# Side work of a two-layer kernel told out at other points of its feed-forward stage: from the gate/up blocks into the first down-projection

## The chip, the cores and the metric

The kernel runs on one core of one Trainium2 chip. The metric is the device time of one execution in microseconds (us), lower is better. Five engines are named as in the profile: PE (TensorE matmul; PEld its weight loads), DVE (VectorE), ACT (ScalarE), POOL (GpSimd) and SP (SyncE, which here issues the DMA transfers).

## The reference, cut to what matters

Two transformer layers run one after the other on 512 tokens of width 1024. The change lies in the feed-forward part of the first layer and in two pieces of the second layer that depend on no activation:

```
# first layer, feed-forward part, width 2816
h = rms_norm(x, ffn_norm)
x = x + (silu(h @ w_ffn_gate) * (h @ w_ffn_up)) @ w_ffn_down
...
# second layer: modulation, three rows of 1024 from the conditioning vector c
mod = silu(c) @ w_ada + b_ada
shift, scale, gate = split(mod, 3)
# second layer: matrices of the state-space mixer, from its parameters alone
lam_bar = exp(lam * dt); b_bar = ((lam_bar - 1) / lam) * b; ...
```

The kernel calls the first piece `modulation()` and the second `s5_params()`. Both are needed only after the feed-forward part: scale and shift in its last normalization, the gate and the matrices later.

## The kernel before, in words

All large products use a three-matmul split: an f32 operand becomes a rounded part (hi) and a remainder (lo), and hi·hi, hi·lo and lo·hi are summed in PSUM (`mm3`, lines 177 to 179). A weight tile is fetched by SP (line 198), cast by ACT to its hi part (line 206) and reduced by POOL to its lo part (line 207). There are three raw buffers and three pairs of hi and lo buffers.

The feed-forward part is cut in two halves of 11 column blocks, 22 blocks m in all (lines 1400 to 1414). One block multiplies the normalized activations hT by 128 columns of the gate weight and by 128 of the up weight, 24 matmuls each, into two of the four PSUM banks tagged `mm`. ACT takes the tanh of the gate bank (line 1405), DVE forms the silu from it (line 1406, the last read of the gate bank), DVE multiplies by the up bank (line 1408, the last read of that bank), and a split writes gT (hi by ACT at line 187, lo by DVE at line 188). After each half a down-projection adds gT times 11 x 128 rows of the down weight to XT: two column blocks of 512 columns, in each of them 11 values of k, for each k the four token tiles t with one bank each, three matmuls per tile. So a column block is 132 matmuls and needs all four `mm` banks at its start. DVE adds the four banks to XT at its end (line 1225). The first half's down-projection is the `add_proj` of line 1414 (through `proj_tok`, line 253), the second's is called later, with a normalization behind it.

Two generators tell out the side work in steps; `some(gen, n)` runs n steps at the point of the program where it is called.

- `modulation()` (line 1270) has 25 steps. For each of three rows n and eight values of k it fetches a 512 KB tile `aw` of w_ada (line 1283, one buffer) and lets DVE multiply and add it into `am` (line 1285 for k = 0, line 1287 for the others, one buffer); call these the products. The step after a row's eighth product first closes that row: `am` is split into two parts in buffers tagged `t4k` (three buffers, lines 184 and 185), PE sums the partitions with four narrow matmuls (line 1295, banks `tp`), DVE adds the bias (line 1296, buffers `t2k`), and SP stores the result to `modd`. Row 0 is closed in step 9, row 1 in step 17, row 2 in step 25.
- `s5_params()` (line 1310) has 11 steps for each of two halves of the groups, 22 in all: Bb, BD and Cm (with four PE transposes of line 1327); two steps of CL; the matmuls of line 1350 with Kp; two steps that copy a table `tk` (t4k buffers) out; two steps of E with one of ET behind each (eight PE transposes of line 1378); and PH, a chain of some forty small DVE products. Nearly all of its DVE work has line 1096 (`cmul`).

Before the change every block m runs one step of `s5_params()` and one step of `modulation()`, two of the latter in blocks 10, 11 and 12 (lines 1411 and 1412). For m < 4 an `issue_after` keeps that work's DVE instructions behind the last one of the normalization ahead of the stage.

The program is written as one sequence. A planner at compile time then puts each instruction in the fixed queue of its engine: an instruction may go ahead of earlier ones as soon as its inputs and its buffer are free by the planner's estimate, and of several that could go, the one written first goes first. Buffers that share a tag (`t2k`, `t4k`, `tp`, `mm`) are handed out by turns. On the chip each engine works through its queue in order and waits by semaphores.

Of the kernel before, what the change touches and what calls it, by code (L numbers as in the profile page):

```python
# [25 lines left out]
NT = 4  # L26
# [62 lines left out]
def row(ap, off, n, parts=128):  # L89
    return bass.AP(tensor=ap.tensor, offset=ap.offset + off, ap=[[0, parts], [1, n]])  # L90
# [60 lines left out]
def tile_hybrid(ctx: ExitStack, tc: tile.TileContext, I, out):  # L151
# [9 lines left out]
    def mm_ps():  # L161
        return ps.tile([128, 512], FT, tag="mm", bufs=4, name="mm")
# [4 lines left out]
    def tp_ps():  # L167
        return ps.tile([128, 512], FT, tag="tp", bufs=2, name="tp")

    def t2k(dt=FT):  # L170
        return at.tile([128, 512], dt, tag="t2k", bufs=4, name="t2k")
# [4 lines left out]
    def mm3(o, a, b, first, last):  # L176
        nc.tensor.matmul(o, a[0], b[0], start=first, stop=False)  # L177
        nc.tensor.matmul(o, a[0], b[1], start=False, stop=False)  # L178
        nc.tensor.matmul(o, a[1], b[0], start=False, stop=last)  # L179

    def split(p, hi, lo, scale=1.0):

        if isinstance(scale, float) and scale == 1.0:
            nc.scalar.copy(hi, p)  # L184
            return nc.vector.tensor_tensor(lo, p, fl(hi), op=OP.subtract)  # L185
        else:
            nc.scalar.activation(hi, p, AF.Copy, scale=scale)  # L187
            return nc.vector.scalar_tensor_tensor(lo, p, scale, fl(hi), op0=OP.mult, op1=OP.subtract)
# [24 lines left out]
    def wl(w, c0, cols, kc=KD, k0=0, dst=None):  # L213
        return wload([(lambda v: v, wcols(w, c0, cols, kc, k0))], kc, cols, dst)

    def proj_t(w, x, kc, m, n0=0, n1=T, bank=mm_ps):

        o = bank()
        for k in range(kc):
            mm3(o[:m, n0:n1], [v[:, k, :m] for v in w], [v[:, k, n0:n1] for v in x], k == 0, k == kc - 1)  # L220
        return o
# [28 lines left out]
            yield  # L250
        return o

    def proj_tok(load, x, kc, kper, cols, tail=0, then=None):


        o = [mm_ps() for _ in range(NT)]
        starts = list(range(0, kc, kper))
        body = len(starts) - tail
        steps = []
        for i, k0 in enumerate(starts):  # L260
            w = load(k0)
            for k in range(k0, min(k0 + kper, kc)):
                steps += [(0 if i < body else 1, k if i < body else t, k, t, w, k - k0) for t in range(NT)]
        for _, _, k, t, w, kw in sorted(steps, key=lambda z: (z[0], z[1])):
            mm3(o[t][:, :cols], [v[:, k, t * 128:(t + 1) * 128] for v in x],
                [v[:, kw, :cols] for v in w], k == 0, k == kc - 1)
            if then and k == kc - 1:
                then(t, o[t])
        return o

    def rsqrt_steps(ss, n, dim, parts=128):
# [35 lines left out]
    def some(gen, n=1 << 30):  # L307
        for _ in range(n):
            if next(gen, gen) is gen:
                return  # L310
# [386 lines left out]
    for j in range(4):  # L697
        w = wl(w_in, C0["iq"] + j * 128, 128)
# [72 lines left out]

    g_q = grow(I["mla_q_norm"], 384)
    o4 = proj_tok(lambda k: wl(w_in, C0["cq"], 384, 2, k), hT, KD, 2, 384)
    todo.add(gates(2))
    for _ in tok_norms(o4, 384, g_q, cqT):
# [6 lines left out]
                 for k in range(3)], 3, 256)  # L782
    qps = [pc.tile([128, T], FR, name=f"qps{h}") for h in range(4)]
    o4 = proj_tok(lambda k: wpe, cqT, 3, 3, 256)
    qpt = []
    qpa = t4k().rearrange("p (t h d) -> p t h d", t=NT, h=4)
# [165 lines left out]
    for h in range(4):  # L952
# [39 lines left out]
        while n <= 256:  # L992
# [23 lines left out]
            if n < 256:  # L1016
                m = 256 // n
# [200 lines left out]
        split(mixed[:, k], *[v[:, k % 4] for v in mx[k // 4]])  # L1218
    mxT = [Rows([m[i] for m in mx], 4) for i in range(2)]

    def add_proj(w, x, kc, tail=0, then=None, last=None):

        for n0 in range(0, D, 512):
            def add(t, o):
                nc.vector.tensor_tensor(XT[:, t, n0:n0 + 512], XT[:, t, n0:n0 + 512], o, op=OP.add)  # L1225
                if then:
                    then(n0 // 512, t)

            proj_tok(lambda k: wl(w, n0, 512, min(2, kc - k), k, last if n0 and k >= kc - 2 else None),
                     x, kc, 2, 512, tail if n0 else 0, add)  # L1230

    hT = hT_tiles()
    g_ffn = grow(I["ffn_norm"], D)
# [23 lines left out]
    w_g, w_u, w_d = I["w_ffn_gate"][0], I["w_ffn_up"][0], I["w_ffn_down"][0]  # L1257
    spare = pmix.tile([128, 2, 2, 1024], FR, tag="mixed", name="spare")
    spare = [[spare[:, i, j] for j in range(2)] for i in range(2)]
    add_proj(I["w_out"][0], mxT, KD, 3, norm_x, spare[1])  # L1260
    first2 = proj_halves([wl(w_g, 0, 128, dst=spare[0]), wl(w_u, 0, 128)], hT)
    stg.close()
# [3 lines left out]
    KH = KF // 2  # L1266
    gT = [pf.tile([128, KH, T], FR, name=f"gT{i}") for i in range(2)]
    modd = dr.tile([24, 128], FT, name="modd")

    def modulation():  # L1270

        cth = pf.tile([128, KD], FT, name="cth")
        nc.scalar.activation(cth, cs, AF.Tanh, scale=0.5)
        nc.vector.scalar_tensor_tensor(cs, cth, 1.0, cs, op0=OP.add, op1=OP.mult)
        nc.vector.tensor_scalar(cs, cs, 0.5, None, op0=OP.mult)
        w_ada = I["w_ada_2"][0].rearrange("(k p) c -> p k c", p=128)
        one = pf.tile([128, 1], FR, name="one")
        nc.vector.tensor_copy(one, ones)
        for n in range(3):
            am = pf.tile([128, D], FT, tag="am", bufs=1, name="am")  # L1280
            for k in range(KD):
                aw = pf.tile([128, 1024], FT, tag="aw", bufs=1, name="aw")
                nc.sync.dma_start(aw, w_ada[:, k, n * D:(n + 1) * D])
                if k == 0:
                    nc.vector.tensor_scalar(am, aw, cs[:, 0:1], None, op0=OP.mult)
                else:
                    nc.vector.scalar_tensor_tensor(am, aw, cs[:, k:k + 1], am, op0=OP.mult, op1=OP.add)  # L1287
                yield
            parts = [at.tile([128, 1024], FR, tag="t4k", bufs=3, name="am") for _ in range(2)]
            split(am, *parts)  # L1290
            for c in (0, 512):
                p, r = tp_ps()[0:1], t2k()[0:1]
                nc.sync.dma_start(r, row(I["b_ada_2"], n * D + c, 512, 1))
                for i, v in enumerate(parts):
                    nc.tensor.matmul(p, one, v[:, c:c + 512], start=i == 0, stop=i == 1)
                nc.vector.tensor_tensor(r, r, p, op=OP.add)
                nc.sync.dma_start(row(modd, n * D + c, 512, 1), r)
# [99 lines left out]
            yield  # L1397

    mod_steps, s5_steps = modulation(), s5_params()
    for half in range(2):  # L1400
        for i in range(KH):
            m = half * KH + i
            pg = proj_t(wl(w_g, m * 128, 128), hT, KD, 128) if m else first2[0]
            th = t2k()
            nc.scalar.activation(th, pg, AF.Tanh, scale=0.5)
            nc.vector.scalar_tensor_tensor(th, th, 1.0, pg, op0=OP.add, op1=OP.mult)  # L1406
            pu = proj_t(wl(w_u, m * 128, 128), hT, KD, 128) if m else first2[1]
            nc.vector.tensor_tensor(th, th, pu, op=OP.mult)  # L1408
            split(th, gT[0][:, i], gT[1][:, i], 0.5)
            with tc.issue_after(at_norm[0].ins) if m < 4 else nullcontext():  # L1410
                some(s5_steps, 1)
                some(mod_steps, 2 if m in (10, 11, 12) else 1)
        if not half:
            add_proj(w_d[:KH * 128], gT, KH)
    some(mod_steps)
    some(s5_steps)
    st5.close()
# [22 lines left out]
    def norm_twice(half, t):  # L1440
# [25 lines left out]
        for k in range(0, KD, 2):  # L1466
# [5 lines left out]
            for kk in range(2):  # L1472
# [3 lines left out]
                at_norm[0] = nc.vector.scalar_tensor_tensor(lo, p[:, kk], sh, fl(hi), op0=OP.add, op1=OP.subtract)  # L1476

    add_proj(w_d[KH * 128:], gT, KH, 3, norm_twice)
    ud = dr.tile([512, T], FT, name="ud")
    us = proj_halves(w_us + [wl(w2, C2["u"] + m * 128, 128) for m in range(2, 3)], h2)  # L1480
# [5 lines left out]
    for t in range(NT):  # L1486
        x = XT[:, t]
# [552 lines left out]
    for n0 in range(0, D, 512):  # L2040
        o4 = proj_tok(lambda k: wl(w_o2, n0, 512, 2, k), mix, 4, 2, 512, n0 // 256)
        for t in range(NT):
# [4 lines left out]
            w = 256 if n0 and t == NT - 1 else 512  # L2047
# [34 lines left out]
```

## Time and profile before

| | us |
|---|---|
| median of 3 runs (lowest to highest) | 1378.11 (1372.89 to 1378.55) |
| profiled execution, its own time | 1378.97 |
| its span, first to last instruction | 1377.2 |
| PE busy | 1279.4 (93%) |
| DVE busy | 858.9 (62%) |
| POOL busy | 640.1 (46%) |
| ACT busy | 551.5 (40%) |

The feed-forward stage with what surrounds it lies at about 600 to 1000 us of the span. The page gives the shares of the engines over the whole span; the views of single stretches (windows, waits by engine, the timeline of one engine) tell which engine waits for which, and where. In a timeline the number in brackets at the end of a row is the idle time of the engine just before, with the instruction that ended it. A busy PE counts matmuls that overlap their neighbours, so the starts of successive matmuls, not their durations, give PE's rate.

### The profile page before, as it was taken

How to read it: one execution, taken by the hardware profiler on the slowest of the kernel's cores; microseconds unless marked ns; L12 is line 12 of the kernel's file. 1: busy time of each engine (PE TensorE's matmuls, PEld its weight loads, DVE VectorE, ACT ScalarE, POOL GpSimd, SP SyncE). 2: the span in 40 equal slices, each digit the busy share in tenths (PEclk: the TensorE clock that was granted, in tenths of full speed). 3: DMA queues.
4: the chain of work that ended last, by engine and by line, in shares of the span. 5: the costliest groups of instructions: out<-in, count | busy, mean ns of one | idle time of the engine just before them, and what ended most of it. 6: DMA issues, size and time to landing. Idle time of an engine off the chain costs nothing. (4 is left out here: it accounts for less than half of the span.)

```text
span 1377.2 us, 18201 instructions
## 1 busy us (share of the span) xinstructions
PE 1279.4 (93%) x6418; PEld 1054.0 (77%) x6418; DVE 858.9 (62%) x1831; ACT 551.5 (40%) x1242; POOL 640.1 (46%) x552
## 2 busy tenths in 40 slices
PE   8989999999989999999998899999989788789998
PEld 6777887777768888878876688887778678677786
DVE  6755897776534346268667516354363758897885
ACT  4554542322234434343423123432343234447772
POOL 3334433333455455554565345554532443547663
PEclk9999999999999999999999899999999898999999
DMA  6252222221423373333765434533325665231233
GB/s 199 71 158 58 63 75 65 62 57 36 116 80 88 86 176 92 123 92 115 224 196 187 143 99 121 169 109 102 113 77 162 185 173 132 69 92 47 77 108 138
DMA packets 201962, 156.16 MB, mean 113 GB/s; under 512 B 27535, under 2 KB 175707, under 8 KB 201869
## 3 DMA queue, kind: packets, MB, share of 16 engines
q1 hardware_dynamic: 201868, 154.98, 38.7%
q8 instruction: 51, 0.84, 0.3%
q14 instruction: 43, 0.34, 0.1%
HBM read 136.58 MB, written 18.37 MB: 113 GB/s over the span
## 5 line engine op out<-in xcount | busy, mean ns | idle before, releaser
L207 POOL TENSOR_TENSOR wlo<-wraw,whi 128x512 fp32r<-128x512 f32 (+4 forms) x388 | 507.1, 1327 | 602.7 <-ACT whi L206 601.4
L206 ACT CAST whi<-wraw 128x512 fp32r<-128x512 f32 (+4 forms) x388 | 212.3, 575 | 366.1 <-issue 217.3
L177 PE MATMUL mm<-hT,whi 128*128 128x512 f32 (+2 forms) x840 | 335.8, 400 | 0.0
L179 PE MATMUL mm<-hT,wlo 128*128 128x512 f32 (+2 forms) x840 | 327.9, 390 | 0.0
L178 PE MATMUL mm<-hT,whi 128*128 128x512 f32 (+2 forms) x840 | 327.7, 390 | 0.0
L179 PEld LDWEIGHTS mm<-hT,wlo 128*128 128x128 f32 x840 | 160.4, 191 | 31.3
L177 PEld LDWEIGHTS mm<-hT,whi 128*128 128x128 f32 x840 | 160.9, 191 | 29.9 <-PE mm L179 0.5
L178 PEld LDWEIGHTS mm<-hT,whi 128*128 128x128 f32 x840 | 161.0, 192 | 28.5 <-issue 0.7
L177 PE MATMUL mm<-whi,gT 128*128 128x512 f32 x176 | 71.7, 408 | 14.5 <-DVE t2k L1406 6.9
L1225 DVE TENSOR_TENSOR XT<-XT,mm 128x512 f32<-128x512 f32 x24 | 16.3, 685 | 99.7 <-PE mm L179 99.6
L178 PE MATMUL mm<-wlo,gT 128*128 128x512 f32 x176 | 71.3, 405 | 0.0
L179 PE MATMUL mm<-whi,gT 128*128 128x512 f32 x176 | 71.2, 405 | 0.0
L177 PE MATMUL mm<-whi,hT 128*128 128x512 f32 (+3 forms) x160 | 60.1, 375 | 0.3 <-ACT hT L184 0.3
L179 PE MATMUL mm<-whi,hT 128*128 128x512 f32 (+3 forms) x160 | 59.3, 371 | 0.9 <-DVE hT L185 0.9
L178 PE MATMUL mm<-wlo,hT 128*128 128x512 f32 (+3 forms) x160 | 59.3, 371 | 0.2 <-POOL wlo L207 0.2
L1287 DVE SCALAR_TENSOR_TENSOR am<-aw,prm,am 128x1024 f32<-128x1024 f32 x21 | 32.4, 1543 | 36.2 <-DMA aw<-in_w_ada_dram 36.2
L185 DVE TENSOR_TENSOR pt4k<-tp,pt4k 128x512 fp32r<-128x512 f32 (+1 forms) x96 | 45.8, 483 | 14.4 <-ACT pt4k L184 13.7
L177 PEld LDWEIGHTS mm<-whi,gT 128*128 128x128 f32 x176 | 34.2, 194 | 24.7 <-DVE t2k L1406 7.3
L184 ACT CAST pt4k<-tp 128x512 fp32r<-128x512 f32 (+1 forms) x96 | 40.1, 421 | 32.0 <-PE tp L387 30.8
L187 ACT ACTIVATE gT<-t2k 128x512 fp32r<-128x512 f32 x22 | 13.9, 631 | 82.3 <-DVE t2k L1408 82.3
L179 PEld LDWEIGHTS mm<-whi,gT 128*128 128x128 f32 x176 | 34.1, 194 | 8.3
L178 PEld LDWEIGHTS mm<-wlo,gT 128*128 128x128 f32 x176 | 34.1, 194 | 7.9
(641 smaller groups left out, 2666.8 us busy)
## 6 DMA issues: line engine op xcount, KB each, us to landing
wraw<-in_w_in_dram SPq DMA_DIRECT2D x70, 512.0 KB
aw<-in_w_ada_dram SPq DMA_DIRECT2D x24, 512.0 KB
wraw<-in_w_ffn_gate_dram SPq DMA_DIRECT2D x22, 512.0 KB
wraw<-in_w_ffn_up_dram SPq DMA_DIRECT2D x22, 512.0 KB
wraw<-in_w_ffn_down_dram SPq DMA_DIRECT2D x20, 512.0 KB
wraw<-in_w_out_dram SPq DMA_DIRECT2D x16, 512.0 KB
PA<-biasd SPq DMA_DIRECT2D x4, 640.0 KB
x<-in_x_dram SPq DMA_DIRECT2D x4, 512.0 KB
```

Of the source, the lines that this page charges most:

```text
L177: nc.tensor.matmul(o, a[0], b[0], start=first, stop=False)
L178: nc.tensor.matmul(o, a[0], b[1], start=False, stop=False)
L179: nc.tensor.matmul(o, a[1], b[0], start=False, stop=last)
L184: nc.scalar.copy(hi, p)
L185: return nc.vector.tensor_tensor(lo, p, fl(hi), op=OP.subtract)
L187: nc.scalar.activation(hi, p, AF.Copy, scale=scale)
L206: nc.scalar.copy(hi[:, d], raw[:, d])
L207: nc.gpsimd.tensor_tensor(lo[:, d], raw[:, d], fl(hi[:, d]), op=OP.subtract)
L1225: nc.vector.tensor_tensor(XT[:, t, n0:n0 + 512], XT[:, t, n0:n0 + 512], o, op=OP.add)
L1287: nc.vector.scalar_tensor_tensor(am, aw, cs[:, k:k + 1], am, op0=OP.mult, op1=OP.add)
```

## The change

In both halves a block runs its steps only if it is not one of the last two of its half (`i < KH - 2`, that is blocks 0 to 8 and 11 to 19). There it runs one step of `s5_params()`, and one of `modulation()` in the second half alone. The first down-projection gets a function that is called after the last token tile of each k: a step of `s5_params()` at k = 1, 5 and 9, and a step of `modulation()` at k = 1 to 10. With two column blocks these are 6 and 20 steps. So the steps of `s5_params()` stand at blocks 0 to 8 (steps 1 to 9), in the down-projection (10 to 15) and at blocks 11 to 17 (16 to 22); those of `modulation()` in the first column block (1 to 10), in the second (11 to 20) and at blocks 11 to 15 (21 to 25). The `issue_after` stays, but it now covers steps of `s5_params()` alone.

```diff
-    def proj_tok(load, x, kc, kper, cols, tail=0, then=None):
+    def proj_tok(load, x, kc, kper, cols, tail=0, then=None, beside=None):
...
             if then and k == kc - 1:
                 then(t, o[t])
+            if beside and t == NT - 1:
+                beside(k)
...
-    def add_proj(w, x, kc, tail=0, then=None, last=None):
+    def add_proj(w, x, kc, tail=0, then=None, last=None, beside=None):
...
-                     x, kc, 2, 512, tail if n0 else 0, add)
+                     x, kc, 2, 512, tail if n0 else 0, add, beside)
...
     mod_steps, s5_steps = modulation(), s5_params()
+
+    def told_down(k):
+        some(s5_steps, 1 if k % 4 == 1 else 0)
+        some(mod_steps, 1 if k else 0)
+
...
             with tc.issue_after(at_norm[0].ins) if m < 4 else nullcontext():
-                some(s5_steps, 1)
-                some(mod_steps, 2 if m in (10, 11, 12) else 1)
+                if i < KH - 2:
+                    some(s5_steps, 1)
+                    some(mod_steps, half)
         if not half:
-            add_proj(w_d[:KH * 128], gT, KH)
+            add_proj(w_d[:KH * 128], gT, KH, beside=told_down)
```

## Rows read from the trace of the kernel before

**Rows 1.** The page, part 1: busy time, share of the span, instructions.

```profile
PE 1279.4 (93%) x6418; PEld 1054.0 (77%) x6418; DVE 858.9 (62%) x1831; ACT 551.5 (40%) x1242; POOL 640.1 (46%) x552
```

**Rows 2.** Waits of PE, 600 to 800 us, then 800 to 980: total, times, longest.

```profile
PE mm L177 <- DVE t2k L1406: 6.9, 1, 6.9
PE mm L177 <- DVE t2k L1408: 3.2, 1, 3.2
...
PE tp L1378 <- DVE E L1096: 2.4, 1, 2.4
PE tp L1378 <- DVE t2k L1296: 1.0, 1, 1.0
...
PE mm L177 <- DVE t2k L1408: 1.5, 1, 1.5
```

**Rows 3.** Windows: stretch, then length; PE, PEld, DVE, ACT, POOL busy; clock, DMA.

```profile
751.67:769.00 17.33, 7.23 (x20) 4.93 (x19) 16.04 (x41) 2.55 (x5) 7.12 (x4) 0.61 0.54 174
...
796.50:824.50 28.00, 28.00 (x121) 22.61 (x120) 0.00 (x0) 5.19 (x10) 11.47 (x9) 1.00 0.34 103
```

**Rows 4.** Timeline of PE at the start of the first down-projection.

```profile
752.84 0.39 PE L179 MATMUL mm<-whi,gT 128*128 128x512 f32 x1
760.10 0.79 PE L177 MATMUL mm<-whi,gT 128*128 128x512 f32 x1 [6.87 <-DVE t2k L1406]
...
764.97 0.79 PE L177 MATMUL mm<-whi,gT 128*128 128x512 f32 x1 [3.23 <-DVE t2k L1408]
...
768.97 0.43 PE L177 MATMUL mm<-whi,gT 128*128 128x512 f32 x1
```

**Rows 5.** Timeline of DVE across the end of the first half.

```profile
747.51 1.28 DVE L1287 SCALAR_TENSOR_TENSOR am<-aw,prm,am 128x1024 f32<-128x1024 f32 x1 [3.25 <-DMA aw<-in_w_ada_dram]
748.72 0.68 DVE L1408 TENSOR_TENSOR t2k<-t2k,mm 128x512 f32<-128x512 f32 x1
...
752.65 1.35 DVE L1287 SCALAR_TENSOR_TENSOR am<-aw,prm,am 128x1024 f32<-128x1024 f32 x1 [2.28 <-DMA aw<-in_w_ada_dram]
...
757.58 1.24 DVE L1096 TENSOR_TENSOR t2k<-PH 128x8 f32<-128x8 f32 x1
...
759.36 0.68 DVE L1406 SCALAR_TENSOR_TENSOR t2k<-t2k,mm 128x512 f32<-128x512 f32 x1
...
764.23 0.68 DVE L1408 TENSOR_TENSOR t2k<-t2k,mm 128x512 f32<-128x512 f32 x1
```

**Rows 6.** Waits of all engines, 625 to 800 us: the products' own row.

```profile
DVE am L1287 <- DMA aw<-in_w_ada_dram: 36.2, 16, 4.9
```

**Rows 7.** Side work against its place in the program: groups by line, and timeline rows.

```profile
L1283 SPq DMA_DIRECT2D aw<-in_w_ada_dram x24: 327/328/413, 630.1 to 781.4; - x24
L1285 DVE TENSOR_SCALAR am<-aw,prm x3: 642/1405/1683, 636.6 to 742.0; 128x1024 f32<-128x1024 f32 x3
L1287 DVE SCALAR_TENSOR_TENSOR am<-aw,prm,am x21: 1273/1286/2310, 647.3 to 786.0; 128x1024 f32<-128x1024 f32 x21
L184 ACT CAST am<-am x3: 1044/1052/1054, 685.3 to 880.1; 128x1024 fp32r<-128x1024 f32 x3
...
630.51 0.43 SPq L1424 DMA_DIRECT2D g_fin<-in_final_norm_dram  x1
...
860.33 1.26 DVE L1296 TENSOR_TENSOR t2k<-t2k,tp 1x512 f32<-1x512 f32 x2
```

**Rows 8.** Timeline of PE around the wait of the transposes in the first half.

```profile
713.34 0.98 PE L1378 MATMUL tp<-ident,E 128*128 128x128 f32 x7 [2.38 <-DVE E L1096]
714.08 0.48 PE L177 MATMUL mm<-hT,whi 128*128 128x512 f32 x1
...
717.76 0.43 PE L177 MATMUL mm<-hT,whi 128*128 128x512 f32 x1
```

**Rows 9.** Timeline of DVE: the additions to XT at both column ends.

```profile
793.71 2.79 DVE L1225 TENSOR_TENSOR XT<-XT,mm 128x512 f32<-128x512 f32 x4 [6.46 <-PE mm L179]
...
824.51 2.79 DVE L1225 TENSOR_TENSOR XT<-XT,mm 128x512 f32<-128x512 f32 x4 [28.01 <-PE mm L179]
```

## The prediction, made before the changed kernel ran

> **What bounds the kernel now.** I read the shares of the engines first: PE is busy for 93% of the span, DVE for 62% [rows 1]. So a change that neither adds nor removes matmuls can only pay where PE waits, and the second view is the list of PE's waits from 600 to 980 us. The reader is to see that those that matter here all name DVE, and that all but one lie in the first half of the feed-forward stage; from 800 to 980 us there is a single one, of 1.5 us [rows 2]. The third view is the table of windows: where the first down-projection starts, PE is busy for 7.23 of 17.33 us at a granted clock of 0.61, a mixture of the two levels 1.2 and 2.4 GHz, while DVE is busy for 16.04 us; in the second column block of the same projection PE is full at clock 1.00 and DVE does nothing for 28 us [rows 3]. Work that crowds DVE at the one place would be free at the other.
>
> The timeline of PE prices the crowding. At full clock matmuls start 0.233 us apart (28.00 us for 120, counting one of the two that straddle an edge [rows 3]). After the matmul at 752.84 the next was due at 753.07; instead twelve matmuls were started from 760.10 on before the one at 768.97, when the rate was back [rows 4]. That is 15.9 us for 12 x 0.233 = 2.8 us of work: **13.1 us lost**, 6.87 + 3.23 = 10.1 in the two waits and 3.0 at the low clock behind them. The two waits are for PSUM banks: the projection's third and fourth bank are the gate and up banks of block 10, free when DVE has read them (lines 1406 and 1408).
>
> The timeline of DVE says why it was late. Ahead of these two reads, at 759.36 and 764.23, its queue holds products that sit waiting for their weights, 3.25 and 2.28 us, and the beginning of PH [rows 5]. Over the stage the products wait 36.2 us in 16 places [rows 6], and whatever stands behind them waits too.
>
> **Does the order follow the program?** Only in part, and the sum hangs on it. The products run far ahead of their place: the last one stands in block 20, after the first down-projection, and ran at 786.0; a transfer written behind the whole stage, g_fin, was issued at 630.51. What takes a buffer shared by turns stays at its place: row 1 was split before row 2's first product at 742.0, but its bias was added at 860.33, by block 13; row 2's products ended at 786.0 + 1.3 = 787.3 and its split came at 880.1 [rows 7]. So moving the calls will not by itself move the products of rows 0 and 1: they will still fill the first half. But row 2's products need `am`, free only when row 1 is split; that needs two of three t4k buffers, two of which row 0 holds until its closing matmuls; and row 0's closing now stands at k = 9 of the first column block, behind block 10 in the turns for t2k and tp. I therefore expect the eight products of row 2 at about 775 to 825, no longer at 742 to 787.
>
> **The change part by part**, against the profiled execution's own 1378.97 us (span 1377.2 us and 1.8 us around it; 0.9 us over the median of 1378.11).
>
> 1. *Row 2's products leave the end of the first half.* From 742.0 to 759.36 DVE loses the product of 742.0 (up to 1.68 us), the waits of 3.25 and 2.28 and the products of 1.28 and 1.35 [rows 5, 7]: 9.8 us. The gate bank of block 10 would be read at 749.5, before PE asks at 753.07: margin 3.5 us, out of which PH, which may still be placed here, needs nothing more than it does now. One more product (1.29) lies between the two reads, so the up bank would be read at 764.23 - 11.1 = 753.1 and be free at 753.8, which is when PE asks for it. Row 0's closing also leaves (two additions, 1.26 us). I take the whole 13.1; the bounds are 0 (another waiting product takes the place) and 13.1.
> 2. *Row 0's closing leaves the first half*: PE's wait of 1.0 us for line 1296 goes [rows 2]. Bounds 0 and 1.0; I take 1.0.
> 3. *PH and row 2's closing leave block 21.* The wait of 1.5 us at the start of the second down-projection goes [rows 2], as both now end by block 17. Bounds 0 and 1.5; I take 1.5.
> 4. *E of step 8.* PE waits 2.38 us for it in mid-half, and then starts nine matmuls in 3.68 us, 1.6 over their 2.1: 4.0 us in all [rows 8]. The step stays at block 7 and the products around it stay too, in a new order. I take 0, with bounds of 4.0 either way.
> 5. *New work beside the down-projection*: steps 10 to 15 and the products. DVE's idle time hides their busy time (all eight products are 10.3 us, against 28 us idle in one column block [rows 3, 7]), but not an ill-placed wait: the four additions to XT at each column end free PE's banks [rows 9], and one of them behind a waiting product holds PE. The mean wait is 36.2 / 16 = 2.3 us, the longest 4.9 [rows 6]. I take one mean wait, +2.3; bounds 0 and 13.1 per column end, the price that rows 4 show for a delay of that kind with its clock.
> 6. *SP's queue.* The transfers of w_ada, the two bias loads and two stores of each closing and the stores of steps 10 to 15 now pass the twelve down-projection weights. They cost nothing as long as three raw buffers cover them; no PE wait in rows 2 names a transfer. If the cover went, the price would be that of a late weight, bounded by the 4.9 us of rows 6 each. Taken as 0.
> 7. *The lost `issue_after` of the first steps of modulation* costs nothing: their buffers came free at 630, and the first product ran at 636.6 [rows 7]. PE's side work (transposes, closing matmuls) is only moved.
>
> The waiting products share SBUF with POOL's weight splits: the product takes 1273 ns at best and 2310 at worst [rows 7]. The Trainium skill's page "SBUF — State Buffer", section "Who interferes with whom", says that a VectorE instruction with two SBUF inputs and a GpSimd instruction that reads SBUF exclude each other for a whole instruction, which speaks against putting products next to a column end: with one such lengthening of about 1.0 us at each of the two, an estimate from that rule, the sum would be 2 us less gain. The fastest and slowest product agree with it.
>
> Sum: -13.1 - 1.0 - 1.5 + 0 + 2.3 = -13.3, so 1365.7 us; **1366 us**, 12 below the median.
>
> **The rivals.**
>
> - *Nothing runs ahead any more.* If the steps stay where they are written, the first half has no products at all, and E is in time too: -13.1 - 1.0 - 1.5 - 4.0 = -19.6, 1359 us. For it: the shared buffers keep to their turns; against it: the products and g_fin do not [rows 7]. Chance 0.13.
> - *The order hardly changes.* If row 0 is closed early after all (its products are done in time, and it only needs a turn), row 2's products run at the end of the half as before, and only terms 2 and 3 or less are left: 1377 us. For it: the planner lets ready work go ahead; against it: 94 us between row 2's last product and its split. It is also the case in which the change does not do what it says. Chance 0.22.
> - *Slower: the additions to XT wait behind products.* Row 2's products come one per 5 to 6 us and would span both column ends. If at each end one stands ahead of the additions while its weights are late, and steps 13 and 14 (CL) behind it, PE stops with all banks full, at 13.1 us an end [rows 4]: 26.2 - 15.6 = +10.6, 1390 us. It decides once the two ends together cost over 15.6 us. Against it: before, products ran into the first column block too, up to 786.0 [rows 7], and the additions at 793.71 waited for PE alone [rows 9]. Chance 0.13.
>
> **How the numbers follow.** My forecast has 0.52, 1366 us. About 0.5% (7 us) is what a measurement of this kernel can tell from no change. Faster by more than that (below 1371.2) are nearly all of my case (0.50), all of the first rival and a little of the second: 0.64. Within 0.5% are most of the second and the rest of mine: 0.21. Slower (above 1385) are the third and a remainder: 0.15. The range goes from 1357, just under the first rival, to 1378, above the second, and leaves out the third and a little below.
>
> **What would show it.** Right: in the timeline of DVE the products of row 2 start after 765; PE's waits for lines 1406 and 1408 near 752 are gone and the granted clock there is 1.00; the wait of 1.5 us before the second down-projection is gone; row 0's bias is added in the first down-projection. Wrong: products with waits still between the reads of blocks 9 and 10; new PE waits for line 1225 in the first down-projection; or a PE wait there for a transfer or for CL.

## The result, and the profile after

The changed kernel takes **1386.1 us** (median of 7 runs, 1383.55 to 1389.70), beside 1377.99 us of the kernel before on the same chip: ratio 1.0068, 95% interval 1.0048 to 1.0089. It is slower by 0.7%, 8 us, where 12 us less were forecast, and lies above the range. The profiled execution of after took 1387.16 us, its span is 1385.4 us against 1377.2. Code behind the inserted lines has numbers higher by 2 up to line 1400 (1225 is now 1227, 1287 is 1289), by 7 in the blocks (1406 is 1413, 1408 is 1415).

The busy times are those of [rows 1] within 2 us, but for POOL.

The page of after, part 1:

```profile
PE 1280.3 (92%) x6418; PEld 1052.8 (76%) x6418; DVE 856.9 (62%) x1831; ACT 552.0 (40%) x1242; POOL 648.1 (47%) x552
```

POOL has the same 552 instructions and is busy for 8 us more (640.1 before). That is a first hint: they last longer, and something must stand in their way.

Waits of PE after, from 600 to 800 us and then from 800 to 980 (total, times, longest), the answer to [rows 2]:

```profile
PE mm L177 <- DVE t2k L1415: 4.6, 1, 4.6
PE tp L1380 <- DVE E L1098: 2.7, 1, 2.7
...
PE mm L177 <- DVE t2k L1413: 1.8, 1, 1.8
...
PE mm L177 <- DVE XT L1227: 9.0, 1, 9.0
PE mm L178 <- POOL wlo L207: 1.9, 1, 1.9
```

The waits of 1.0 us (row 0's bias) and of 1.5 us (second down-projection) are gone. The two waits for block 10's banks have only shrunk, from 6.9 and 3.2 to 1.8 and 4.6. New are 9.0 us for the additions to XT, and 1.9 us for a weight's lo part.

Windows of after (stretch, length; PE, PEld, DVE, ACT, POOL busy; clock, DMA). The first two are the stretches of [rows 3], the third is the end of the first down-projection:

```profile
751.67:769.00 17.33, 10.96 (x39) 8.22 (x38) 12.08 (x36) 3.01 (x6) 5.09 (x5) 0.70 0.29 99
796.50:824.50 28.00, 26.08 (x112) 20.31 (x111) 12.14 (x13) 4.04 (x7) 21.97 (x9) 1.00 0.42 119
828.00:845.00 17.00, 7.99 (x24) 6.01 (x23) 7.55 (x10) 6.18 (x18) 4.90 (x4) 0.70 0.61 185
```

The reader is to see a trade in the first and third rows, and the mark of its cause in the second: POOL's nine instructions there took 11.47 us before and take 21.97 us now, with DVE no longer idle beside them.

The timeline of PE after, at both places:

```profile
751.94 0.39 PE L179 MATMUL mm<-whi,gT 128*128 128x512 f32 x1
754.13 0.50 PE L177 MATMUL mm<-whi,gT 128*128 128x512 f32 x1 [1.80 <-DVE t2k L1413]
...
759.67 0.79 PE L177 MATMUL mm<-whi,gT 128*128 128x512 f32 x1 [4.57 <-DVE t2k L1415]
...
765.75 0.40 PE L179 MATMUL mm<-whi,gT 128*128 128x512 f32 x1
...
828.87 0.40 PE L179 MATMUL mm<-whi,gT 128*128 128x512 f32 x1
838.27 0.76 PE L177 MATMUL mm<-hT,whi 128*128 128x512 f32 x1 [9.01 <-DVE XT L1227]
...
844.30 0.40 PE L179 MATMUL mm<-hT,wlo 128*128 128x512 f32 x1
```

Priced as in the prediction, at 0.233 us a matmul: the first place was due at 752.17 and back at rate at 765.75, with 17 matmuls between: 13.58 - 3.97 = **9.6 us lost** (13.1 before). The second was due at 829.10 and back at 844.30, with 14 matmuls between: 15.20 - 3.27 = **11.9 us lost** (nothing before).

The same account by stages. The length of a stage is the distance between the starts of the first matmuls of it and of the next one, read from each profile's timeline of PE. Ahead of the stage the profiles already differ by up to 4 us, so the lengths are compared, not the times. The lower half is for the experiments below.

| kernel | first half | first down-projection | second half | second down-projection | ratio to before (95%) |
|---|---|---|---|---|---|
| before | 136.2 | 74.7 | 125.1 | 72.6 | 1 |
| after | 135.1 | **87.5** | 125.3 | 70.9 | 1.0068 (1.0048 to 1.0089) |
| e1_no_cl | 134.7 | 73.7 | 123.7 | 73.1 | 0.9968 (0.9955 to 0.9982) |
| e2_row2_late | 133.3 | 74.3 | 123.5 | 71.8 | 0.9971 (0.9959 to 0.9984) |
| e3_s5_held | 134.1 | 76.6 | 124.7 | 70.9 | 0.9995 (0.9984 to 1.0006) |
| e4_both | 135.9 | 65.8 | 123.5 | 70.7 | 0.9906 (0.9883 to 0.9928) |
| e5_cl_held | 135.6 | 74.9 | 123.8 | 71.1 | 0.9970 (0.9958 to 0.9981) |
| e6_mod_only | 136.1 | 73.3 | 124.2 | 75.2 | 0.9999 (0.9985 to 1.0013) |
| e7_s5_only | 131.0 | 72.6 | 123.5 | 71.8 | 0.9932 (0.9917 to 0.9947) |
| e8_before_held | 135.0 | **61.6** | 125.1 | 71.1 | 0.9887 (0.9868 to 0.9905) |
| e9_before_ph | 136.0 | 68.7 | 125.1 | 72.6 | 0.9950 (0.9932 to 0.9968) |
| e10_before_row2 | 136.6 | 68.0 | 125.1 | 72.7 | 0.9958 (0.9944 to 0.9971) |
| e11_cl_behind | 135.0 | 77.1 | 124.0 | 70.6 | 0.9998 (0.9986 to 1.0010) |
| e12_s5_held | 132.7 | 65.1 | 123.5 | 72.3 | 0.9902 (0.9887 to 0.9917) |

After against before: -1.1 + 12.8 + 0.2 - 1.7 = 10.2 us, all of it lost in the first down-projection, whose 264 matmuls alone are 264 x 0.2333 = 61.6 us. At the end of the span 8.2 us are left; the 2 us that come back later were not followed. Of the 12.8 us, -3.5 are the first place, 9.2 the second (the other 2.7 of its 11.9 us, the low clock behind the wait, fall into the second half), 2.2 the wait for wlo with the slow start behind it; the other 4.8 are matmuls and transposes of the side work, moved into this stage.

**Why the first place stays.** The timeline of DVE after, at the end of the first half, with PH between the two reads:

```profile
748.48 1.26 DVE L1098 TENSOR_TENSOR t2k<-PH 128x8 f32<-128x8 f32 x1
749.77 1.21 DVE L1098 TENSOR_TENSOR PH<-PH,t2k 128x8 f32<-128x8 f32 x1
...
752.16 0.17 DVE L1098 TENSOR_TENSOR PH<-PH 128x16 f32<-128x16 f32 x1
...
753.40 0.68 DVE L1413 SCALAR_TENSOR_TENSOR t2k<-t2k,mm 128x512 f32<-128x512 f32 x1
...
758.93 0.68 DVE L1415 TENSOR_TENSOR t2k<-t2k,mm 128x512 f32<-128x512 f32 x1
...
803.81 1.20 DVE L185 TENSOR_TENSOR am<-am 128x1024 fp32r<-128x1024 f32 x1
...
805.55 0.74 DVE L1287 TENSOR_SCALAR am<-aw,prm 128x1024 f32<-128x1024 f32 x1
819.49 2.35 DVE L1289 SCALAR_TENSOR_TENSOR am<-aw,prm,am 128x1024 f32<-128x1024 f32 x1 [13.21 <-DMA aw<-in_w_ada_dram]
...
835.95 1.28 DVE L1289 SCALAR_TENSOR_TENSOR am<-aw,prm,am 128x1024 f32<-128x1024 f32 x1 [4.01 <-DMA aw<-in_w_ada_dram]
...
837.45 2.47 DVE L1227 TENSOR_TENSOR XT<-XT,mm 128x512 f32<-128x512 f32 x4
```

There is no product here any more. PH's first steps multiply 128 x 8 numbers, and four of the first five take 1.2 us each; others of about that size take 0.17. The same fence shows the second place further down: row 1's split at 803.81, row 2's first product at 805.55, its second at 819.49 after 13.21 us of waiting, and the additions to XT, which could have begun near 829, at 837.45 behind the fifth product.

The timeline of POOL after says what the slow ones stood beside:

```profile
744.18 10.50 POOL L207 TENSOR_TENSOR wlo<-wraw,whi 128x512 fp32r<-128x512 f32 x8 [4.43 <-ACT whi L206]
...
784.59 2.54 POOL L207 TENSOR_TENSOR wlo<-wraw,whi 128x512 fp32r<-128x512 f32 x2 [4.30 <-ACT whi L206]
...
794.89 18.78 POOL L207 TENSOR_TENSOR wlo<-wraw,whi 128x512 fp32r<-128x512 f32 x6 [1.33 <-ACT whi L206]
```

Eight splits in a row from 744.18 to 754.68, just where PH's small steps last 1.2 us, about the length of one split (10.50 / 8 = 1.31). And six splits from 794.89 on, beside CL, that take 18.78 us. Their mean of 3.1 us misleads, as the same timeline shows for 794.9 to 807 us and for 807.5 to 813 us alone:

```profile
794.89 12.52 POOL L207 TENSOR_TENSOR wlo<-wraw,whi 128x512 fp32r<-128x512 f32 x1 [1.33 <-ACT whi L206]
...
807.37 6.30 POOL L207 TENSOR_TENSOR wlo<-wraw,whi 128x512 fp32r<-128x512 f32 x5
```

One split took 12.52 us; the five behind it took 6.30 / 5 = 1.26 each, like the two without company (2.54 / 2 = 1.27). From 795.29 to 806.29 DVE worked through CL, row 1's split and row 2's first product without a gap, and POOL's one split ended only behind them, at 807.41. So in the first place DVE's small steps each wait for a split of POOL, and in the second place one split of POOL waits for a whole row of DVE's instructions. The Trainium skill's page "SBUF — State Buffer", section "Who interferes with whom", says that a VectorE instruction with two SBUF inputs contends with a GpSimd instruction that reads SBUF; both rows agree with it.

The timeline of SP after carries the lateness on:

```profile
794.04 0.28 SPq L1299 DMA_DIRECT2D modd<-t2k  x1
808.69 0.35 SPq L198 DMA_DIRECT2D wraw<-in_w_ffn_down_dram  x1
...
812.84 2.23 SPq L1285 DMA_DIRECT2D aw<-in_w_ada_dram  x1
```

SP stood from 794.3 to 808.69 in front of a weight's transfer, whose raw buffer is free only when POOL has split the tile in it: the late split ended at 807.41, the next one 1.3 us behind it. The `aw` behind it was free to be filled from 806.3 on (the product of 805.55 with its 0.74) and was issued at 812.84.

### The profile page after: what moved, and what is told of

Same layout as the page of the kernel before. It is cut to its first block, busy times and chain, and to the rows that moved or that the text cites. A ratio compares the mean times of both kernels' runs of the same rounds, so it can differ in the third digit from the quotient of the medians.

```text
span 1385.4 us, 18212 instructions
## 1 busy us (share of the span) xinstructions
PE 1280.3 (92%) x6418; PEld 1052.8 (76%) x6418; DVE 856.9 (62%) x1831; ACT 552.0 (40%) x1242; POOL 648.1 (47%) x552
## 4 chain that ended last, share of the span: by engine, by line
PE 53%; DVE 18%; DMA 6%; issue 4%; ACT 2%; POOL 1%; SPq 0%; DVEq 0%; ACTq 0%; POOLq 0%
PE mm L177 14%; PE mm L179 14%; PE mm L178 14%; DMA aw<-in_w_ada_dram 5%; DVE am L1289 2%; PE tp L389 1%; PE s L1001 1%; DVE t2k L1098 1%; POOL wlo L207 1%; PE mm L376 1%; DVE bF L892 1%; DVE rq_u L290 1%; PE s L410 1%; PE mm L375 1%; DVE rq_u L288 1%
## 5 line engine op out<-in xcount | busy, mean ns | idle before, releaser
L207 POOL TENSOR_TENSOR wlo<-wraw,whi 128x512 fp32r<-128x512 f32 (+4 forms) x388 | 513.7, 1344 | 605.6 <-ACT whi L206 604.5
L185 DVE TENSOR_TENSOR pt4k<-tp,pt4k 128x512 fp32r<-128x512 f32 (+1 forms) x96 | 45.9, 484 | 14.5 <-ACT pt4k L184 13.9
L187 ACT ACTIVATE gT<-t2k 128x512 fp32r<-128x512 f32 x22 | 13.9, 631 | 73.0 <-DVE t2k L1415 73.0
```

Source lines behind the costliest of these rows:

```text
L207: nc.gpsimd.tensor_tensor(lo[:, d], raw[:, d], fl(hi[:, d]), op=OP.subtract)
```

## The experiments

The theory, T: CL's instructions on DVE stand beside POOL's splits and ahead of row 1's closing. So row 2's products start late, one split and with it SP and the weights of the products are late, and the additions to XT stand behind products that wait. (The expectations below still speak of splits of 3.1 us each; that is the mean of the one long split and its five neighbours.) At the start of the down-projection PH alone is the rest of the old loss. Rival A: the products ahead of the additions hold PE by their own pace, with or without CL.

**e1_no_cl**, the steps of `s5_params()` out of the second column block:

```diff
-        some(s5_steps, 1 if k % 4 == 1 else 0)
+        at_k.append(k)
+        some(s5_steps, 1 if k % 4 == 1 and len(at_k) <= KH else 0)
...
+                if i < KH - 2 + half:
+                    some(s5_steps, 1)
                 if i < KH - 2:
-                    some(s5_steps, 1)
                     some(mod_steps, half)
```

> The changed kernel with the steps of s5_params taken out of the second column block of the first down-projection (the two steps of CL and the matmuls of line 1352 go to the blocks behind it); modulation stays where the change put it. Theory T (CL on DVE beside POOL's splits stretches each split from 1.3 to 3.1 us, so SP is held by a raw buffer and the transfers of aw come late): splits of 1.3 us, products on time, the 9.0 us wait of PE for the additions to XT falls to 2 us or less, so 12.0 us come back: 1372 to 1376 us. Rival A (eight products of row 2 ahead of the additions are enough by themselves): the wait stays at 5 us or more and the time at 1380 or more. The 4.6 us wait at the start of the down-projection stays with either.

Measured 1372.36 us. No wait for XT is left in the first down-projection, the waits at its start are 4.6 and 1.8 us as before. This supports T, but not cleanly: the planner still pulled four of CL's instructions into the column block. e5 repeats it with a hold.

**e2_row2_late**, row 2's products behind the last addition, CL where the change put it. Row 1's closing goes with them, as it stands in the same step as the first of them; so it does in every hold of row 2 below.

```diff
+                at_add[0] = nc.vector.tensor_tensor(XT[:, t, n0:n0 + 512], XT[:, t, n0:n0 + 512], o, op=OP.add)
...
+        at_k.append(k)
...
-        some(mod_steps, 1 if k else 0)
+        some(mod_steps, 1 if k and len(at_k) < KH + 8 else 0)
...
-                    some(mod_steps, half)
+                    if half:
+                        with tc.issue_after(at_add[0].ins):
+                            some(mod_steps, 1)
```

> The changed kernel with the products of row 2 held behind the last addition to XT of the first down-projection (told out at blocks 11 to 19); CL stays beside the second column block. Both theories expect the 9.0 us wait for the additions and the low clock behind it to go, 12.0 us: 1374 us, between 1371 and 1377. If PE still waits 4 us or more in the second column block, CL alone (or the late weights behind POOL's splits of 3.1 us) holds it, and the products were not the carrier. Waits of PE for wlo (1.9 and 1.3 us) stay, as CL and the splits still run side by side.

Measured 1372.37 us. PE's only wait over 0.4 us from 740 to 850 us is one of 5.8 us at the start. Seven splits in a row still take 18.09 us, 10.2 of them in one split beside CL, and yet PE waits for no wlo, against what was expected. So a split that stands for 10 us need not reach PE by itself; the long wait, that for XT, needs the products to carry the delay.

**e3_s5_held** and **e4_both**. e3 holds the steps of `s5_params()` in the first down-projection behind block 10; e4 has this and e2's hold.

```diff
-            split(th, gT[0][:, i], gT[1][:, i], 0.5)
+            at_gt[0] = split(th, gT[0][:, i], gT[1][:, i], 0.5)
...
-        some(s5_steps, 1 if k % 4 == 1 else 0)
+        with tc.issue_after(at_gt[0].ins):
+            some(s5_steps, 1 if k % 4 == 1 else 0)
```

> The changed kernel with the steps of s5_params told in the first down-projection (10 to 15, PH the second of them) held behind block 10's last DVE instruction. Theory: PH is now what stands between the two reads of block 10's gate and up banks; with it gone the two waits (1.8 and 4.6 us) and the low clock behind them go, 9.6 us: 1376.5 us if nothing later changes. Rival: another filler (products) takes the gap, the waits stay within 2 us of what they were and the time within 3 us of 1386. The 9.0 us wait in the second column block stays with either; it may grow if PH shoves the products later.

> Both holds: row 2's products behind the last addition to XT, and the steps of s5_params behind block 10. If the two losses are independent, 1386.1 - 12.0 - 9.6 = 1364.5 us, within 4 us; no PE wait over 2.5 us between 740 and 860 us. If they are one loss that moves (removing one enlarges the other), 1374 us or more.

e3 measured 1375.92 us, 10 below after where 9.6 were expected. Waits of PE in e3, 740 to 850 us:

```profile
PE mm L177 <- DVE XT L1227: 7.7, 1, 7.7
PE mm L178 <- POOL wlo L207: 1.9, 1, 1.9
```

Both waits at the start are gone, so PH was all that was left there; the wait for XT stays. e4 measured 1363.66 us against an expected 1364.5: the two losses are independent, and without them the same moves are faster than the kernel before by 0.9%.

**e5_cl_held**, e1 with a clean hold: CL and the matmuls of line 1352 behind the last addition, row 2's products untouched.

```diff
+                if i < KH - 2 + half:
+                    with tc.issue_after(at_add[0].ins) if half else nullcontext():
+                        some(s5_steps, 1)
                 if i < KH - 2:
-                    some(s5_steps, 1)
                     some(mod_steps, half)
```

> The changed kernel with the steps of s5_params of its second column block (CL and the matmuls of line 1352) told behind that block and held behind its last addition to XT; the eight products of row 2 stay told in the down-projection, and five of them stand ahead of the first addition. Theory T (CL beside POOL's splits makes the weights late, SP stands, the products are late, the additions wait): with CL gone POOL's splits in the first half of the block fall under 2 us each, the first transfer of aw behind row 1 is issued more than 8 us earlier, PE waits 2 us or less for XT, and 12.0 us come back: 1372 to 1376. Rival A (the products ahead of the additions hold PE by their own number and pace): PE still waits 5 us or more for XT and the time stays at 1381 or more.

Measured 1371.66 us. The timeline of DVE in e5:

```profile
797.66 1.00 DVE L1289 TENSOR_SCALAR am<-aw,prm 128x1024 f32<-128x1024 f32 x1
805.55 1.29 DVE L1291 SCALAR_TENSOR_TENSOR am<-aw,prm,am 128x1024 f32<-128x1024 f32 x1 [6.88 <-DMA aw<-in_w_ada_dram]
...
822.68 1.29 DVE L1291 SCALAR_TENSOR_TENSOR am<-aw,prm,am 128x1024 f32<-128x1024 f32 x1 [2.47 <-DMA aw<-in_w_ada_dram]
825.70 1.38 DVE L1229 TENSOR_TENSOR XT<-XT,mm 128x512 f32<-128x512 f32 x2 [1.73 <-PE mm L179]
```

Five products stand ahead of the first addition, as in after, but they are done in time: the addition at 825.70 waits for PE, not for a transfer, and PE doesn't wait for XT at all. The second product runs 13.9 us earlier (805.55 against 819.49; 15.9 counted from the start of the stage), the first `aw` behind row 1 is issued at 800.74. No split from 790 to 825 us took over 2.14 us. T holds and rival A falls: at the normal pace the same products in the same place cost nothing. With e2 it follows that **CL and row 2's products hold PE only together**.

**e11_cl_behind** tries to split CL's part in two: CL stays in the column block, but behind row 1's closing and row 2's first product.

```diff
-                    nc.vector.tensor_scalar(am, aw, cs[:, 0:1], None, op0=OP.mult)
+                    at_p[0] = nc.vector.tensor_scalar(am, aw, cs[:, 0:1], None, op0=OP.mult)
...
-        some(s5_steps, 1 if k % 4 == 1 else 0)
+        at_k.append(k)
         some(mod_steps, 1 if k else 0)
+        if len(at_k) <= KH:
+            some(s5_steps, 1 if k % 4 == 1 else 0)
+        elif k > 7:
+            with tc.issue_after(at_p[0].ins):
+                some(s5_steps, 1)
```

> The changed kernel with CL kept beside the second column block, but held behind row 1's closing and row 2's first product; the products stay told as they are, and five of them stand ahead of the first addition. It splits the lateness of the products in two. In the changed kernel the first transfer of aw of row 2's second product was issued 14.1 us later, counted from the start of the down-projection, than with CL gone: 9.9 us because CL stands ahead of the closing on DVE, 4.2 us because SP stood behind a late raw buffer. If DVE's order is the larger part, the first product of row 2 runs 8 us or more earlier, PE waits 2.5 us or less for XT, and the time is 1372 to 1377. If CL beside POOL's splits is enough wherever it stands (late raw buffers, SP standing), the later transfers are 8 us and more apart, PE waits 5 us or more, and the time is 1380 or more.

Measured 1376.47 us. The timeline of DVE in e11:

```profile
793.55 1.38 DVE L1289 TENSOR_SCALAR am<-aw,prm 128x1024 f32<-128x1024 f32 x1
...
812.89 1.27 DVE L1291 SCALAR_TENSOR_TENSOR am<-aw,prm,am 128x1024 f32<-128x1024 f32 x1
819.98 1.29 DVE L1291 SCALAR_TENSOR_TENSOR am<-aw,prm,am 128x1024 f32<-128x1024 f32 x1 [5.82 <-DMA aw<-in_w_ada_dram]
...
827.07 1.27 DVE L1227 TENSOR_TENSOR XT<-XT,mm 128x512 f32<-128x512 f32 x2
```

Row 2's first product runs 12.0 us earlier, PE's wait for XT is 2.8 us, and the stage lasts 77.1 us: 10.4 of the 12.6 us between after (87.5) and e5 (74.9) came back. The 2.8 us stay, with the next three transfers of `aw` still 7 to 10 us apart. Both outcomes were partly right. But e11 doesn't change DVE's order alone: its longest split beside CL took 4.88 us and not 12.52, so SP stood less too. That the place in DVE's queue is the larger part is read from the traces and not shown by a run of its own: counted from the start of the stage, the transfer for row 2's second product was issued 14.1 us later in after than in e5, 9.9 of them because the first product ran later, 4.2 because SP came to it later.

**e6_mod_only** and **e7_s5_only**, each half of the change alone:

```diff
-        some(s5_steps, 1 if k % 4 == 1 else 0)
         some(mod_steps, 1 if k else 0)
...
+                some(s5_steps, 1)
                 if i < KH - 2:
-                    some(s5_steps, 1)
                     some(mod_steps, half)
```

and, for e7:

```diff
         some(s5_steps, 1 if k % 4 == 1 else 0)
-        some(mod_steps, 1 if k else 0)
...
                 if i < KH - 2:
                     some(s5_steps, 1)
-                    some(mod_steps, half)
+                some(mod_steps, 2 if m in (10, 11, 12) else 1)
```

> Half of the change: modulation told as in the changed kernel, s5_params as before the change (a step in each block, none in the down-projection). CL then stands in the second half, PH still between the two reads of block 10. Theory T: no PE wait over 2 us for XT, the waits at the start of the down-projection as in the changed kernel (6.4 us, 9.6 lost), the wait of 1.5 us at the second down-projection back: 1386.1 - 12.0 + 1.5 = 1375.6, between 1372 and 1378. Rival A (the products alone): 1383 or more.

> The other half: s5_params told as in the changed kernel, modulation as before the change. Row 2's products then come behind the first down-projection, CL beside its second column block. Theory T: without a product ahead of the additions late weights cost PE no more than the 3.2 us that it waits for wlo in the changed kernel; the loss of 9.6 us at the start stays (PH): 1375, between 1372 and 1379. Rival B (CL beside POOL's splits is enough to hold the additions): PE waits 4 us or more for XT, 1382 or more.

e6 measured 1375.55 us, no different from before; e7 1367.14 us, better than expected. Neither has a wait for XT over 0.5 us there. That e7 is below its bound is partly the first half (131.0 us, 5.2 less than before; PE's waits from 600 to 740 us fell from 6.0 to 3.7 us); the rest of it was not followed. Beside each other: modulation alone 0.0%, `s5_params()` alone -0.7%, both +0.7%. The loss is an interplay; no half has it.

**e8_before_held, e9_before_ph, e10_before_row2**: the kernel before, nothing moved in the program, with holds. e9 has the first one below, e10 the second, e8 both.

```diff
-            split(th, gT[0][:, i], gT[1][:, i], 0.5)
+            gt_lo = split(th, gT[0][:, i], gT[1][:, i], 0.5)
+            if m == KH - 1:
+                at_gt = gt_lo
...
-                some(s5_steps, 1)
-                some(mod_steps, 2 if m in (10, 11, 12) else 1)
+                with tc.issue_after(at_gt.ins) if m >= KH - 1 else nullcontext():
+                    some(s5_steps, 1)
+                with tc.issue_after(at_add[0].ins) if m > 12 else nullcontext():
+                    some(mod_steps, 2 if m in (10, 11, 12) else 1)
```

> The kernel before the change with nothing moved in the program and two holds: the steps of s5_params from block 10 on behind that block's last DVE instruction, and row 2's steps of modulation behind the last addition to XT of the first down-projection. Theory: all 13.1 us of the two waits at the start of the first down-projection go, and nothing new waits: 1378.0 - 13.1 = 1364.9, within 4 us. Rival: the place where work is told matters beyond these two pieces (rows 0 and 1 and the other steps): 1370 or more.

> The kernel before the change with the steps of s5_params from block 10 on (PH first) held behind that block's last DVE instruction; row 2's products stay at the end of the first half. By the prediction's first step the products' waits and durations are 9.8 us of the delay, so most of the 13.1 us stay: 1375 or more. By the theory that PH between the two reads is the larger part: 5 to 10 us come back, 1368 to 1373.

> The kernel before the change with row 2's steps of modulation held behind the last addition to XT of the first down-projection; PH stays between block 10's reads. By the prediction's first step the products were the delay: 9.8 to 13.1 us come back, 1365 to 1368. By the theory that PH alone still holds the banks: 9.6 us stay lost as in the changed kernel, only 3.5 come back: 1374.5, between 1372 and 1377.

e9 measured 1369.80 us, e10 1370.57, e8 **1361.51**. e9's 6.5 us lie within what the theory on PH expected. e10 lies between what its two theories expected: 5.8 us came back, where the prediction's own step wanted 9.8 or more and the other 3.5. Waits of PE at the start of the down-projection in e9, the products alone:

```profile
PE mm L177 <- DVE t2k L1408: 2.5, 1, 2.5
PE mm L177 <- DVE t2k L1406: 1.2, 1, 1.2
```

and in e10, PH alone:

```profile
PE mm L177 <- DVE t2k L1410: 4.6, 1, 4.6
```

By the lengths of the stage over 61.6 us, both together lose 13.1 us, the products alone 7.1 (with 1.1 for XT at the first column end), PH alone 6.4, and without either nothing is lost. 7.1 and 6.4 make 13.5: on the kernel before the two delays nearly add up. Windows of e8, over the start and the rest of the stage:

```profile
752.00:766.00 14.00, 14.00 (x62) 11.29 (x61) 12.77 (x48) 3.96 (x7) 7.49 (x6) 1.00 0.24 79
766.00:814.00 48.00, 48.00 (x207) 38.67 (x207) 13.35 (x24) 9.30 (x17) 20.95 (x17) 1.00 0.34 104
```

PE is busy throughout at clock 1.00, with PH running beside it from 754.6 on.

**e12_s5_held**, the better half (e7) with both holds, as a search for the fastest version:

```diff
+        with tc.issue_after(at_gt[0].ins):
+            some(s5_steps, 1 if k % 4 == 1 else 0)
...
-                    some(mod_steps, half)
+                with tc.issue_after(at_add[0].ins) if m > 12 else nullcontext():
+                    some(mod_steps, 2 if m in (10, 11, 12) else 1)
```

> The half of the change that moves s5_params alone, with two holds: the steps told in the first down-projection behind block 10's last DVE instruction, row 2's products behind the last addition to XT. It looks for a version faster than the kernel before with its two holds (1361.5 us). The half alone gave 1367.1; its first down-projection lasted 72.6 us against 61.6 us with nothing in the way, and some 2 to 4 us of that are transposes that PE does there. With the wait of 5.0 us and its low clock gone, 7 to 9 us come back: 1360, between 1357 and 1363. If another stall takes its place, 1365 or more.

Measured 1362.92 us, inside what was expected and not below e8. e4, e8 and e12 (ratios 0.9906, 0.9887 and 0.9902, with intervals that overlap) all beat both kernels by about 1%; which of them is fastest the runs don't tell. e8 gets there with no work moved in the program.

Not tried: a second buffer for `aw`, or a fourth raw buffer, which would test SP's part by itself. How the loss at the second place divides between DVE's order, POOL's late split and SP is therefore told by the traces alone.

## Why the prediction was wrong

The sign was wrong. Two steps failed, and both for the same neglect: the instructions that remain were left with the durations and the places they had.

1. *Row 2's products leave* (13.1 us taken, 3.5 measured). They left, as forecast, and no product stands near block 10 any more. The step that failed is "margin 3.5 us, out of which PH, which may still be placed here, needs nothing more than it does now". I forecast the reads at 749.5 and 753.1; they came at 753.40 and 758.93. With the products gone PH moved up beside eight splits in a row, where four of its first five steps cost 1.2 us instead of 0.17, and the rest of the chain still lay between the reads. [rows 5] had the warning: the one step of PH that it shows took 1.24 us for 128 x 8. e10 shows what the step was worth on the kernel before: 6.7 us of the stage, half of the 13.1; e9 gives 6.0 to PH. Together that is 12.7 of the 13.1, all of which I had given to the products. In after the first place lost 3.2 us more than in e10: the gate bank's wait of 1.8, which e10 doesn't have, as only two of PH's steps take 1.2 us there, and 1.4 more at the low clock.
2. *Row 0's closing* (1.0) and 3. *block 21* (1.5) were right: both waits are gone, and the second down-projection lasts 1.7 us less. 4. *E* was right within 0.3 us (2.7 against 2.4).
5. *New work beside the down-projection* (2.3 taken, 11.9 measured, within the bounds of 0 to 13.1 for each end). The first column end cost nothing, the second nearly the upper bound. I priced the late products by the mean wait of the first half, 2.3 us; what came was one wait of 13.21 us, because CL put row 1's closing off and, through POOL's late split, SP. I had forecast the products at 775 to 825; they ran from 805.55 to 857.7, and even without CL (e5) the first came at 797.66. I had looked at the products' pace and at DVE's idle time, and not at what CL, the largest piece of DVE work moved into this stage, does to POOL and to the order of the queue.
6. *SP's queue* (0 taken) failed too, in a smaller way. "They cost nothing as long as three raw buffers cover them" was right as a condition, and the cover went: SP stood for 14.4 us in front of one weight, PE waited 1.9 us for a lo part, and 4.2 of the 14.1 us by which a product's transfer was late against e5 are SP's by the trace.
7. *The lost `issue_after`* cost nothing that shows.

The Trainium skill's rule on shared SBUF access (page and section as above) stood in the prediction with 2 us. The mechanism was right and the size was not: it was applied to two products at the column ends, while the instructions that it hit were PH's small ones (about 1 us each, four of the first five) and one of POOL's splits beside CL (12.52 - 1.27 = 11 us). "For a whole instruction" fell short there: this split stood through a row of them.

*The rivals.* "Nothing runs ahead" and "the order hardly changes" were wrong: row 2's products moved to 805 us and later. The third rival named the place and the actors, the additions behind a late product and CL beside them, but put CL behind the products, not ahead of them, and priced two ends at 26.2 us; one end happened, at 11.9. Its point of decision, 15.6 us, rested on the full gains of steps 1 to 3. With the 6.0 us that these really gave (3.5 + 1.0 + 1.5), one end was enough. What spoke against it, that the additions at 793.71 waited for PE alone [rows 9], held for a stage without CL in it.

## What to carry to other kernels

When several pieces of side work stand ahead of the instruction that frees the bottleneck's buffer, taking away one of them gives back only its own share: price each alone before summing, and give what remains its new neighbours and their cost. Side work told into the idle time of an engine wants an order as well as a time: here two holds, side work behind the last read of the banks and behind the additions, were worth 1% with nothing moved, while moving the work without them lost 0.7%. Two harmless moves can cost together, so a change in two halves is best measured as four kernels.

## What the runs showed of the hardware that was not expected

- A small DVE product of two SBUF inputs pays for the POOL instruction beside it: 128 x 8 took 1.21 to 1.26 us beside back-to-back splits and 0.17 us with POOL idle (e8), seven times as long. In after each of the four slow steps ended 0.03 to 0.04 us behind the end of a split; together they ate the margin of 3.5 us.
- In the other direction one POOL instruction can stand through a whole row of DVE's: a split of 128 x 512 took 12.52 us, while some thirteen DVE instructions without a gap between them ran, and 1.27 us alone. Single splits of 10.2 to 12.5 us stand beside CL in after, e2, e3 and e4. In e7 the same instructions of CL and the splits took turns, and both paid: splits up to 2.15 us, CL's up to 2.16 us instead of 1.03. What decides between the two was not tested. In e2 and e4 the long split cost PE no wait; in after it held SP through the raw buffers.
- What PE loses behind a wait hardly grows with the wait: 6.4 us of waits at the start in after lost 9.6, 9.0 us at the column end lost 11.9, and 4.6 us in e10 lost 6.4, so 1.8 to 3.2 us came on top of short and long ones alike. The granted clock over both stretches of after was 0.70, a mixture of 1.2 and 2.4 GHz; in e8, without the waits, it was 1.00. What comes on top differs between runs with the same waits (6.4 us in after, e1, e5 and e11): e1 and e11 lost 1.2 to 1.4 us less than after and e5, so lengths of the stage that differ by no more than that tell nothing.
